# Two-pass put-back of expert rows: 0/1 matrix, weights applied at eviction, 14-unit spacing of whole units

## Chip, cores and metric

The kernel runs on one core of a Trainium2 chip. The metric is the device time of one execution in microseconds (us). A timed run is one number; a profiled execution also has a span, from its first to its last instruction, and a trace. Five engines work side by side: TensorE (PE in the rows; its weight loads stand apart as PEld), VectorE (DVE), ScalarE (ACT), GpSimd (POOL) and SyncE (SP), whose queue starts the transfers of the weights.

## The reference, cut to what matters

Two blocks run one after the other on 256 tokens of 1024 features. The change lies in the last part of the second block, a mixture of 32 experts: each token picks one group of eight experts, and in it two experts, whose outputs are added with two weights.

```python
def _hierarchical_moe(h, w_group, w_expert, w_gate, w_up, w_down):
    n, d = h.shape                                   # 256 tokens, 1024
    group_prob = jax.nn.softmax((h @ w_group).astype(jnp.float32), axis=-1)
    group = jnp.argmax(group_prob, axis=-1)
    group_gate = jnp.take_along_axis(group_prob, group[:, None], axis=1)
    ...
    top_p, top_local = lax.top_k(jax.nn.softmax(exp_logits, axis=-1), TOP_K)
    top_p = top_p / jnp.sum(top_p, axis=-1, keepdims=True)
    weight = (group_gate * top_p).reshape(-1)
    ...
    def expert_block(args):
        xb, e = args
        return (jax.nn.silu(xb @ w_gate[e]) * (xb @ w_up[e])) @ w_down[e]

    y = lax.map(expert_block, (buf.reshape(n_blocks, MOE_BLOCK, d), block_expert)).reshape(cap, d)
    contrib = y[dest] * w_sorted[:, None].astype(y.dtype)
    return jnp.zeros((n, d), y.dtype).at[tok_sorted].add(contrib)

# in second_block, after it:
    x = x + gate_ffn[:, None, :] * y
    return _rmsnorm(x, g_final)
```

## The kernel before, in words

**Units.** All weights are laid out as units of 128x2048 float32 (1 MB). SP's queue loads them in the order of `PLAN` (L304), into tiles called `raw`. An expert has six: two each of `eg` (gate), `eu` (up) and `ed` (down), so the 32 experts have 192. A unit is split before use: ACT writes its rounded part `hi` (a copy to the type fp32r, L221), DVE the rest `lo` (L348), and PE multiplies with both (`convert_unit`, `rows_times`). A *whole* unit is not split: PE reads `raw` itself in full float32, and ACT and DVE have nothing to do for it. Function `whole` picks them among the experts' units: index 9 and every 20th after it, nine units in all.

**Slots.** One pool of `NS = 18` tiles of 1 MB holds raw units, split units (two each), the tokens' rows (`hth`, `htl`), the state `x` and the experts' outputs. `prefetch` starts a load when fewer than `st["cap"]` raw units are held (6 in this stage) and a slot is free. `take_unit` splits up to two units ahead of the one in use.

**Pairs.** Experts go in pairs p, each with 32 slots per expert. For pair p the loop runs `gate_up` (PE banks `pe`), `hidden` (bank `pT`, then the product with silu, `sgm` and `hsz`), and `down` (banks `pd`), where `down` of pair p-1 stands between the `gate_up` of pair p and p+1. ACT evicts `pe` and later `pd` to a tile `gy` (two pairs share a 1 MB slot). `gather` (bank `pg`) fetches the tokens' rows for four pairs at a time.

**Put-back.** After every fourth pair `put_back` adds the four pairs' rows to the tokens. For each of eight feature blocks and each pair, PE multiplies 128 rows of `gy` with `wsel`, a 128x256 matrix that holds a token's weight in the row of its slot and nought elsewhere, into bank `py`, all in float32; DVE adds the result, scaled by `mod`, to `x` (L1598). `put_weights` makes `wsel` two pairs earlier: DVE writes it by tokens (`gw`), PE transposes it (bank `pw`, L1502), ACT evicts it (`ws`). There are put-backs of four, four, four, three and one pair; the last is in the tail, ahead of the final norm.

**Order.** Work that is not tied to a unit is a generator in the list `bg`; `pull` takes one step of it at each half unit, `post` puts an eviction some half units later, and `drain` runs out what is left. The framework then settles where each engine's instructions stand.

Of the kernel before, what the change touches and what calls it, by code (L numbers as in the profile page):

```python
# [213 lines left out]
def block_kernel(ctx: ExitStack, tc: tile.TileContext, A, out):  # L214
# [5 lines left out]
    def act(out, in_, func, **k):  # L220
        ins = S.activation(out, in_, func, **k).ins  # L221
        last["act" if func in (AF.Copy, AF.Identity, AF.Square, AF.Abs) else "func"] = ins
        return ins
# [12 lines left out]
    def mm(*a, **k):  # L236
        last["mm"] = T.matmul(*a, **k).ins  # L237
# [13 lines left out]
    def unit(name, dt=F32):  # L251
        live[0] += 1
        assert live[0] <= NS, (name, live)
        return units.tile([P, 2048], dt, name=name, tag="u")

    def free(n=1):
        live[0] -= n
# [4 lines left out]
    def t512(name, dt=F32):  # L262
        return tpool[0].tile([P, 512], dt, name=name, tag="t")
# [7 lines left out]
    def k2v(t):  # L271
        return t.rearrange("p (k t) -> p k t", k=2)
# [17 lines left out]
    def whole(u):  # L290

        if u < MOE0:
            return PLAN[u][0] == "v" or PLAN[u][0] == "conv" and PLAN[u][1] in (2, 5)
        m = u - MOE0
        return m < NU - MOE0 - 4 and m % 20 == 9

    def prefetch(upto=-1):
        while st["dma"] < NU and ((len(raw) < st["cap"] and live[0] < NS) or st["dma"] <= upto):
# [104 lines left out]
    def post(fn, n=1):  # L403
        due.append((st["step"] + n, fn))
# [35 lines left out]
    def drain():  # L440
        while bg or bg2:
            pull(1000)
# [843 lines left out]
    first.close()  # L1286
    moe = ctx.enter_context(ExitStack())
    pairs = moe.enter_context(tc.tile_pool(name="pairs", bufs=3, reuse_waits="tile"))
    tpool[0] = moe.enter_context(tc.tile_pool(name="wide2", bufs=5, reuse_waits="tile"))
    st["mconv"] = MOE0  # L1290
    convert_unit(2)
    acc = ps("ss")
# [159 lines left out]
    def choose(g):  # L1452

        oh = ohs[g] = [pairs.tile([P, 256], F32R, name="oh", tag="oh", bufs=4) for tt in range(2)]
        for tt in range(2):
            t1 = t256("oh1")
            V.tensor_scalar(t1, slot, slg[g][:, 0, tt:tt + 1], None, op0=OP.is_equal)
            last["oh"] = V.scalar_tensor_tensor(oh[tt], slot, slg[g][:, 1, tt:tt + 1], t1,
                                                op0=OP.is_equal, op1=OP.add).ins
            yield  # L1460
# [16 lines left out]
            post(keep, 1)  # L1477
            yield

    def put_weights(g):  # L1480

        gw = [t512("gw") for tt in range(2)]
        for tt in range(2):
            t = [t256("gw1") for i in range(2)]
            for i in range(2):
                V.tensor_scalar(t[i], slot, slg[g][:, i, tt:tt + 1], wt[:, i, tt:tt + 1],
                                op0=OP.is_equal, op1=OP.mult)
            g4 = gw[tt].rearrange("p (e i r) -> p e i r", e=8, i=2)
            t3 = [v.rearrange("p (e r) -> p e r", e=8) for v in t]
            for i in range(2):  # L1490
                V.tensor_tensor(g4[:, :, i], t3[0], t3[1], op=OP.add)
            yield
            yield
        for _ in range(6):
            yield
        wsel[g] = pairs.tile([P, 1024], F32, name="ws", tag="ws", bufs=1).rearrange("p (q t) -> p q t", q=4)
        for q2 in range(2):
            p = ps("pw")
            for i in range(2):
                for tt in range(2):  # L1500
                    q = 2 * q2 + i
                    T.transpose(p[:, i * 256 + tt * 128:i * 256 + (tt + 1) * 128],  # L1502
                                gw[tt][:, q * 128:(q + 1) * 128], ident)
            post(lambda p=p, q2=q2: act(wsel[g][:, 2 * q2:2 * q2 + 2].rearrange("p q t -> p (q t)"), p,
                                                 AF.Copy), 2)
            yield

    gy = {}

# [6 lines left out]
                       start=a and j == 0, stop=z and j == len(ws) - 1, skip_group_check=True)  # L1516
        return run

    pes, gyu = {}, {}

    def window(t, e):
        return t[:, (e % 2) * 64:(e % 2) * 64 + 128]
# [1 line left out]
    def gate_up(e):  # L1524
        x4 = xs[e // 4 % 2][:, :, e // 2 % 2]
        q, odd = e // 2, e % 2 == 1
        if not odd:
            pes[q] = [ps("pe"), ps("pe")]
        for i, nm in enumerate(("eg", "eu")):
            p = pes[q][i]  # L1530
            for k2 in range(2):
                for ws in take_unit(nm, e, k2):
                    rows_times([(p, window(x4[:, 4 * k2 + k], e), k, not odd and k2 + k == 0, odd and k2 + k == 4)
                                for k in range(4)])(ws)
        if odd:
            if q % 2 == 0:
                g = unit("gy")
                gy[q], gy[q + 1] = g[:, :1024], g[:, 1024:]
            for i in range(2):
                post(lambda i=i, p=pes[q][i]: act(gy[q][:, i * 512:(i + 1) * 512], p, AF.Copy), i + 2)  # L1540

    def hidden(q):

        t = gy[q]
        p = ps("pT")
        for f in range(8):
            mm(p[:, f * 64:(f + 1) * 64], t[:, f * 128:(f + 1) * 128], fold, start=True, stop=True)
        sg = t256("sgm")
        hs = hsz[q % 2]
        sv = sg.rearrange("p (f e r) -> p f e r", f=4, e=2)  # L1550
        ho = hs.rearrange("p f (h i r) -> p f h i r", h=3, i=2)

        def product():
            act(sg, p[:, 0:256], AF.Silu)
            V.tensor_mul(sg, p[:, 256:512], sg)

        def parts():
            act(ho[:, :, 0:3:2, 0], sv, AF.Copy)
            V.tensor_sub(ho[:, :, 0:3:2, 1], sv, ho[:, :, 0:3:2, 0])  # L1559
        post(product, 2)  # L1560
        post(parts, 4)
        return hs
# [3 lines left out]
    def down(e, hs):  # L1566
        odd = e % 2 == 1
        if not odd:
            pds[:] = [ps("pd"), ps("pd")]
        for k2 in range(2):  # L1570
            for ws in take_unit("ed", e, k2):
                rows_times([(pds[n], window(hs[:, 2 * k2 + i], e), 2 * i + n, not odd and k2 + i == 0,
                             odd and k2 + i == 2) for i in range(2) for n in range(2)])(ws)
        if odd:
            y = gy[e // 2]

            def keep(pd=list(pds)):
                for n in range(2):
                    if n and e == NE - 1:
                        V.tensor_copy(y[:, n * 512:(n + 1) * 512], pd[n])  # L1580
                    else:
                        act(y[:, n * 512:(n + 1) * 512], pd[n], AF.Copy)
            post(keep, 2)

    def put_back(qs, after=None):

        for f2 in range(4):
            p = ps("py")
            for i in range(2):
                f = 2 * f2 + i  # L1590
                for n, q in enumerate(qs):
                    mm(p[:, i * 256:(i + 1) * 256], gy[q][:, f * 128:(f + 1) * 128],
                       wsel[q // 4][:, q % 4], start=n == 0, stop=n == len(qs) - 1)

            def add(f2=f2, p=p):
                for i in range(2):
                    f = 2 * f2 + i
                    V.scalar_tensor_tensor(x[:, f], p[:, i * 256:(i + 1) * 256], mod[:, 40 + f:41 + f], x[:, f],  # L1598
                                           op0=OP.mult, op1=OP.add)
            if after:  # L1600
                after(add)
            else:
                post(add, 3)
            yield
        for q in qs:
            gy.pop(q)
            if q % 2:
                free()

    st["hold"] = held  # L1610
    st["cap"] = 6
# [8 lines left out]
    with tc.issue_after(last["oh"]):  # L1620
        weights()
    for p in range(NE // 2 + 1):
        if p < NE // 2:
            gate_up(2 * p)
        if p:
            if p == NE // 2:
                flush()
                drain()
                flush()
                st["order"] = 0  # L1630
            hs = hidden(p - 1)
            if p == NE // 2:
                flush()
        if p < NE // 2:
            gate_up(2 * p + 1)
            if p % 4 == 3 and p // 4 < 3:
                drain()
                bg.append(gather(p // 4 + 1))
                st["bg"] = 2
            if p % 4 == 2:  # L1640
                bg.append(put_weights(p // 4))
                if p // 4 < 3:
                    bg.append(choose(p // 4 + 1))
        if p:
            for e in (2 * p - 2, 2 * p - 1):
                down(e, hs)
            if st["bg"] == 2:
                drain()
                st["bg"] = 1
            if p % 4 == 0 and p < NE // 2:  # L1650
                post(lambda p=p: bg.insert(0, put_back([p - 4, p - 3, p - 2, p - 1])), 3)
            elif p == NE // 2 - 1:
                post(lambda p=p: bg.insert(0, put_back([p - 3, p - 2, p - 1])), 3)
    flush()
# [127 lines left out]
```

## Time and profile before

| what | us |
|---|---|
| timed runs, median of 3 (lowest, highest) | 1255.14 (1254.77, 1258.93) |
| the profiled execution's own time | 1256.86 |
| its span | 1255.1 |
| PE busy in the span | 1193.1 (95%) |
| DVE busy | 1016.1 (81%) |
| ACT busy | 789.7 (63%) |

Shares over the whole span mix stages that have different limits. The experts take the last 515 us or so (from about 740), and that stage is read by stretches: for each, the busy time of every engine, the share of time in which the DMA engines moved data, and the rate in GB/s. The mean granted TensorE clock of the span is 0.979 of full speed.

### The profile page before, as it was taken

How to read it: one execution, taken by the hardware profiler on the slowest of the kernel's cores; microseconds unless marked ns; L12 is line 12 of the kernel's file. 1: busy time of each engine (PE TensorE's matmuls, PEld its weight loads, DVE VectorE, ACT ScalarE, POOL GpSimd, SP SyncE). 2: the span in 40 equal slices, each digit the busy share in tenths (PEclk: the TensorE clock that was granted, in tenths of full speed). 3: DMA queues.
4: the chain of work that ended last, by engine and by line, in shares of the span. 5: the costliest groups of instructions: out<-in, count | busy, mean ns of one | idle time of the engine just before them, and what ended most of it. 6: DMA issues, size and time to landing. Idle time of an engine off the chain costs nothing.

```text
span 1255.1 us, 18668 instructions
## 1 busy us (share of the span) xinstructions
PE 1193.1 (95%) x7396; PEld 1040.2 (83%) x7396; DVE 1016.1 (81%) x1212; ACT 789.7 (63%) x908; POOL 102.0 (8%) x106
## 2 busy tenths in 40 slices
PE   7989899999999999988999999999999999999996
PEld 6984899999999999978898977777777776778774
DVE  6796799977798988676746689998898979888985
ACT  6465545465654444455455478897778867876873
POOL 1769200210000000000000000000000000000000
PEclk8999899999999999988899989999999999999998
DMA  9634347436877897423106229999999989998971
GB/s 362 265 110 181 113 173 269 159 115 270 348 287 299 339 336 285 194 101 135 68 8 263 101 93 424 421 421 421 370 421 421 421 322 424 421 417 323 423 319 36
DMA packets 48620, 341.20 MB, mean 272 GB/s; under 512 B 5392, under 2 KB 5648, under 8 KB 7824
## 3 DMA queue, kind: packets, MB, share of 16 engines
q1 hardware_dynamic: 47664, 337.65, 68.0%
q10 hardware_dynamic: 864, 2.31, 0.5%
q8 instruction: 60, 0.98, 0.3%
q14 instruction: 32, 0.26, 0.1%
HBM read 338.88 MB, written 1.05 MB: 271 GB/s over the span
## 4 chain that ended last, share of the span: by engine, by line
PE 70%; DVE 14%; ACT 8%; issue 5%; POOL 2%; DMA 1%; SPq 0%; DVEq 0%; ACTq 0%; POOLq 0%
PE pe L237 12%; DVE lo L348 7%; PE pd L237 5%; PE pbr L237 5%; PE fo L237 5%; PE pfg L237 5%; PE pfu L237 5%; PE py L237 4%; PE pq L237 4%; PE po L237 4%; PE pgt L237 4%; ACT hi L221 4%; PE pc L237 2%; PE z L237 2%; PE pg L237 2%
## 5 line engine op out<-in xcount | busy, mean ns | idle before, releaser
L221 ACT ACTIVATE hi<-raw 128x1024 fp32r<-128x1024 f32 (+1 forms) x379 | 549.8, 1471 | 306.3 <-issue 54.2
L348 DVE TENSOR_TENSOR lo<-raw,hi 128x2048 fp32r<-128x2048 f32 (+1 forms) x185 | 410.9, 2262 | 50.2 <-ACT hi L221 37.2
L327 DVE TENSOR_TENSOR lo<-raw,hi 128x1024 fp32r<-128x1024 f32 x194 | 243.3, 1262 | 87.1 <-ACT hi L221 83.1
L237 PE MATMUL pe<-lo,xs 128*128 128x512 f32 x488 | 136.4, 404 | 9.5 <-DVE lo L348 9.1
L237 PE MATMUL pe<-hi,xs 128*128 128x512 f32 x488 | 136.4, 403 | 1.0 <-ACT hi L221 0.7
L237 PEld LDWEIGHTS pe<-lo,xs 128*128 128x128 f32 x488 | 89.0, 188 | 36.7 <-DVE lo L348 18.7
L237 PEld LDWEIGHTS pe<-hi,xs 128*128 128x128 f32 x488 | 90.4, 188 | 25.5 <-ACT hi L221 3.0
L650 DVE SCALAR_TENSOR_TENSOR ca<-ch,par,ca 128x255 f32<-128x255 f32 (+25 forms) x180 | 94.0, 555 | 1.0
L237 PE MATMUL pd<-lo,hsz 128*128 128x512 f32 x244 | 69.0, 404 | 4.0 <-DVE lo L348 3.0
L237 PE MATMUL pd<-hi,hsz 128*128 128x512 f32 x244 | 68.3, 401 | 1.2 <-DVE hsz L1559 1.2
L237 PEld LDWEIGHTS pd<-lo,hsz 128*128 128x128 f32 x244 | 43.4, 188 | 20.7 <-DVE lo L348 12.7
L237 PE MATMUL py<-ws,gy 128*128 128x256 f32 x256 | 57.4, 380 | 2.2 <-ACT gy L221 2.2
L237 PE MATMUL pgt<-nh,hi 128*128 128x256 f32 x192 | 55.8, 290 | 1.9 <-ACT vt L221 1.9
L237 PEld LDWEIGHTS pd<-hi,hsz 128*128 128x128 f32 x244 | 45.9, 188 | 13.5 <-issue 3.0
L316 DVE SCALAR_TENSOR_TENSOR raw<-raw,aux 128x1024 f32<-128x1024 f32 x48 | 56.8, 1218 | 0.0
L237 PEld LDWEIGHTS py<-ws,gy 128*128 128x128 f32 x256 | 48.4, 190 | 10.0 <-ACT gy L221 3.1
L641 POOL TENSOR_TENSOR ca<-ca,tap 128x255 f32<-128x255 f32 (+29 forms) x60 | 54.0, 901 | 21.4 <-ACT tap L221 17.7
L237 PE MATMUL pgt<-nh,lo 128*128 128x256 f32 x192 | 55.3, 288 | 0.0
L237 PE MATMUL pgt<-nl,hi 128*128 128x256 f32 x192 | 55.1, 287 | 0.0
L237 PE MATMUL pfg<-xh,hi 128*128 128x256 f32 x176 | 49.9, 284 | 0.0
L237 PE MATMUL pfg<-xl,hi 128*128 128x256 f32 x176 | 49.7, 283 | 0.0
L237 PE MATMUL pfg<-xh,lo 128*128 128x256 f32 x176 | 49.7, 282 | 0.0
(347 smaller groups left out, 2866.2 us busy)
## 6 DMA issues: line engine op xcount, KB each, us to landing
raw<-in_ws_dram SPq DMA_DIRECT2D x318, 1024.0 KB, 8.6
x<-in_xt_dram SPq DMA_DIRECT2D x4, 256.0 KB, 4.5
raw<-in_ws_dram SPq DMA_DIRECT2D x2, 512.0 KB, 9.0
out_dram<-xo SPq DMA_DIRECT2D x4, 256.0 KB, 2.9
aux<-in_sguw_dram ACTq DMA_DIRECT2D x1, 512.0 KB, 9.5
aux<-in_cnt_dram SPq DMA_DIRECT2D x1, 512.0 KB, 12.6
aux<-in_sgub_dram ACTq DMA_DIRECT2D x1, 512.0 KB, 3.8
aux<-in_cvec_dram ACTq DMA_DIRECT2D x1, 512.0 KB, 4.8
```

Of the source, the lines that this page charges most:

```text
L221: ins = S.activation(out, in_, func, **k).ins
L237: last["mm"] = T.matmul(*a, **k).ins
L316: V.scalar_tensor_tensor(r, r, 1.0, cond["c"], op0=OP.mult, op1=OP.mult, accum_out=mod[:, col:col + 1])
L327: st["lo"] = V.tensor_sub(lo, r, hi).ins
L348: st["lo"] = V.tensor_sub(lo[:, c], raw[u][:, c], hi[:, c]).ins
L641: G.tensor_tensor(ca[:, j, d:], ca[:, j, d:], t[:, :256 - d], op=OP.add)
L650: V.scalar_tensor_tensor(ca[:, j, d:], ch[:, j, :256 - d], w(30 - d), ca[:, j, d:], op0=OP.mult, op1=OP.add)
```

## The change

`wsel` becomes a matrix of noughts and ones of type fp32r. The weight of a row, summed over the tokens, goes to a column `wrow`, and each pair's `pd` is multiplied by it when it is evicted. That eviction makes two parts, as for the weights: ACT writes the rounded half `yh` of a tile `y`, DVE the rest `yl`. `put_back` then multiplies both parts, in fp32r, with the same 0/1 matrix. A pair's `y` now takes a slot of its own from `down` on; the eviction of `pe` goes to a tile `gu` outside the slots.

`put_weights` is cut in two: `weigh` (DVE) runs with the first pair of a group of four, `turn_weights` (PE's transposes, then DVE instead of ACT evicts) right behind the put-back of the group before, because the weights are now needed at the first eviction. The cap on raw units goes 5, 5, 7, 6 with the pair's place in its group. Whole units come every 14th (13 in all). The pool for 128x512 tiles has three buffers instead of five.

```diff
@@ whole
-        return m < NU - MOE0 - 4 and m % 20 == 9
+        return m < NU - MOE0 - 4 and m % 14 == 9
-    tpool[0] = moe.enter_context(tc.tile_pool(name="wide2", bufs=5, reuse_waits="tile"))
+    tpool[0] = moe.enter_context(tc.tile_pool(name="wide2", bufs=3, reuse_waits="tile"))
...
@@ put_weights, now weigh and turn_weights
-            post(lambda p=p, q2=q2: act(wsel[g][:, 2 * q2:2 * q2 + 2].rearrange("p q t -> p (q t)"), p,
-                                                 AF.Copy), 2)
+            def keep(p=p, q2=q2):
+                V.tensor_scalar(wsel[g][:, 2 * q2:2 * q2 + 2].rearrange("p q t -> p (q t)"), p, 0.0, None,
+                                op0=OP.not_equal)
+                V.tensor_reduce(wrow[g][:, 2 * q2:2 * q2 + 2], k2v(p), axis=AX.X, op=OP.add)
+            post(keep, 2)
...
@@ down
-            y = gy[e // 2]
+            q = e // 2
+            y = unit("y", F32R)
+            gy[q] = y[:, :1024], y[:, 1024:]
+            w = wrow[q // 4][:, q % 4:q % 4 + 1]
             def keep(pd=list(pds)):
                 for n in range(2):
-                    if n and e == NE - 1:
-                        V.tensor_copy(y[:, n * 512:(n + 1) * 512], pd[n])
-                    else:
-                        act(y[:, n * 512:(n + 1) * 512], pd[n], AF.Copy)
+                    yh, yl = (v[:, n * 512:(n + 1) * 512] for v in gy[q])
+                    act(yh, pd[n], AF.Copy, scale=w)
+                    V.scalar_tensor_tensor(yl, pd[n], w, yh, op0=OP.mult, op1=OP.subtract)
...
@@ put_back
-                    mm(p[:, i * 256:(i + 1) * 256], gy[q][:, f * 128:(f + 1) * 128],
-                       wsel[q // 4][:, q % 4], start=n == 0, stop=n == len(qs) - 1)
+                    for z, y in enumerate(gy[q]):
+                        mm(p[:, i * 256:(i + 1) * 256], y[:, f * 128:(f + 1) * 128],
+                           wsel[q // 4][:, q % 4], start=n + z == 0, stop=n == len(qs) - 1 and z == 1)
...
@@ the loop over pairs p
+        st["cap"] = (5, 5, 7, 6)[p % 4] if p else 6
+        if p % 4 == 0 and p < NE // 2:
+            bg.append(weigh(p // 4))
+            if not p:
+                bg.append(turn_weights(0))
...
+            if p % 4 == 1:
+                drain()
...
-                post(lambda p=p: bg.insert(0, put_back([p - 4, p - 3, p - 2, p - 1])), 3)
+                def back(p=p):
+                    bg[:0] = [put_back([p - 4, p - 3, p - 2, p - 1]), turn_weights(p // 4)]
+                post(back, 3)
```

The first place is PE at the first put-back (four pairs). Before, with one row for each float32 matrix product (the trace counts two instructions for one):

```order
L237 MATMUL pe<-hi,xs 128x512 x4
L237 MATMUL py<-ws,gy 128x256 x9
L237 MATMUL pe<-lo,xs 128x512 x4
L237 MATMUL pe<-hi,xs 128x512 x4
L237 MATMUL pe<-lo,xs 128x512 x4
L237 MATMUL pe<-hi,xs 128x512 x4
L237 MATMUL py<-ws,gy 128x256 x18
L237 MATMUL pe<-lo,xs 128x512 x4
L237 MATMUL py<-ws,gy 128x256 x5
```

And now:

```order
L237 MATMUL pe<-hi,xs 128x512 x4
L237 MATMUL py<-ws,y 128x256 x18
L237 MATMUL pe<-lo,xs 128x512 x4
L237 MATMUL pe<-hi,xs 128x512 x4
L237 MATMUL pe<-lo,xs 128x512 x4
L237 MATMUL pe<-hi,xs 128x512 x4
L237 MATMUL py<-ws,y 128x256 x10
L237 MATMUL pe<-lo,xs 128x512 x4
L237 MATMUL py<-ws,y 128x256 x18
L1509 MATMUL pw<-cst,gw 128x128 x4
L237 MATMUL py<-ws,y 128x256 x18
```

The 32 float32 products became 64 fp32r ones, and the transposes `pw` of the next four pairs' weights, which stood two pairs later, now stand within them (four more follow a unit later).

The second place is DVE around the same put-back. Before:

```order
L348 TENSOR_TENSOR lo<-raw,hi 128x2048 x9
L1598 SCALAR_TENSOR_TENSOR x<-py,mod,x 128x256 x2
L348 TENSOR_TENSOR lo<-raw,hi 128x2048
L1598 SCALAR_TENSOR_TENSOR x<-py,mod,x 128x256 x4
L348 TENSOR_TENSOR lo<-raw,hi 128x2048
L1598 SCALAR_TENSOR_TENSOR x<-py,mod,x 128x256 x2
L1555 TENSOR_TENSOR sgm<-pT,sgm 128x256
```

And now:

```order
L1597 SCALAR_TENSOR_TENSOR y<-pd,wrow,y 128x512 x2
L348 TENSOR_TENSOR lo<-raw,hi 128x2048 x2
L1614 SCALAR_TENSOR_TENSOR x<-py,mod,x 128x256 x2
L348 TENSOR_TENSOR lo<-raw,hi 128x2048
L1614 SCALAR_TENSOR_TENSOR x<-py,mod,x 128x256 x4
L348 TENSOR_TENSOR lo<-raw,hi 128x2048
L1614 SCALAR_TENSOR_TENSOR x<-py,mod,x 128x256 x2
L1514 TENSOR_SCALAR ws<-pw 128x512
L1516 TENSOR_REDUCE wrow<-pw 128x2
L1514 TENSOR_SCALAR ws<-pw 128x512
L1516 TENSOR_REDUCE wrow<-pw 128x2
```

DVE gains the two parts `yl` of the last pair ahead of the put-back, and four evictions of `pw` behind it; a pair of `y<-pd` stands once in every other pair too.

## Rows read from the trace of the kernel before

**Rows 1.** Windows: stretch, its us; busy PE, PEld, DVE, ACT, POOL; PEclk; DMA share; GB/s.

```profile
739.80:867.70 127.90, 123.65 (x551) 93.86 (x550) 119.01 (x71) 113.14 (x102) 0.00 (x0) 1.00 0.97 401
...
867.70:905.00 37.30, 37.30 (x175) 31.50 (x174) 30.43 (x23) 24.90 (x18) 0.00 (x0) 1.00 0.97 378
905.00:995.00 90.00, 85.21 (x381) 63.66 (x380) 81.85 (x54) 76.10 (x70) 0.00 (x0) 1.00 1.01 421
995.00:1032.00 37.00, 37.00 (x167) 29.96 (x166) 27.22 (x22) 22.13 (x17) 0.00 (x0) 1.00 0.87 338
1032.00:1123.40 91.40, 86.53 (x389) 65.26 (x388) 84.56 (x54) 78.08 (x72) 0.00 (x0) 1.00 1.01 420
1123.40:1160.00 36.60, 36.60 (x172) 30.94 (x172) 28.36 (x22) 23.25 (x18) 0.00 (x0) 1.00 0.86 337
1160.00:1216.00 56.00, 54.27 (x249) 42.63 (x248) 55.15 (x36) 47.01 (x37) 0.00 (x0) 1.00 1.01 420
1216.00:1255.10 39.10, 25.47 (x114) 20.26 (x112) 20.14 (x28) 15.00 (x23) 1.62 (x1) 0.88 0.09 32
```

**Rows 2.** The chain that ended last, at the first put-back: start us, us, what.

```profile
867.89 3.88 PE py L237 x18
871.78 3.73 PE pe L237 x16
875.50 7.77 PE py L237 x36
...
884.20 2.16 PE py L237 x10
```

**Rows 3.** Timeline there, DVE and ACT: in brackets the idle time before and its releaser.

```profile
884.30 2.29 DVE L348 TENSOR_TENSOR lo<-raw,hi 128x2048 fp32r<-128x2048 f32 x1 [4.32 <-issue]
...
886.40 3.77 ACT L221 ACTIVATE hi<-raw 128x2048 fp32r<-128x2048 f32 x2 [5.27 <-PE py L237]
```

**Rows 4.** The chain in the first block: fp32r products of 256 columns, back to back.

```profile
406.77 5.70 PE pfg L237 x48
```

**Rows 5.** Timeline of PE: a whole unit's products, and transposes of the weights.

```profile
1018.87 3.60 PE L237 MATMUL pe<-raw,xs 128*128 128x512 f32 x8
...
811.10 0.82 PE L1502 MATMUL pw<-cst,gw 128*128 128x128 f32 x6
```

**Rows 6.** Groups by form: count, busy us, mean ns of one, idle before.

```profile
L348 DVE TENSOR_TENSOR lo<-raw,hi 128x2048 fp32r<-128x2048 f32 x181 | 406.2, 2286 | 49.5 <-ACT hi L221 36.6 <-issue 10.2 <-PE pd L237 2.2
...
L1486 DVE TENSOR_SCALAR gw<-cst,rt 128x256 f32<-128x256 f32 x16 | 6.2, 405 | 0.0
L1491 DVE TENSOR_TENSOR gw<-gw,gw 128x256 f32<-128x256 f32 x16 | 6.0, 417 | 0.0
...
L1164 DVE TENSOR_REDUCE mx<-z 128x1 f32<-128x256 f32 x8 | 3.3, 413 | 0.0
L1397 DVE SCALAR_TENSOR_TENSOR row<-pT,rt,dg 128x512 f32<-128x512 f32 x4 | 3.0, 745 | 0.0
L1580 DVE COPY gy<-pd 128x512 f32<-128x512 f32 x1 | 0.7, 691 | 4.9 <-PE pd L237 4.9
...
L221 ACT ACTIVATE ws<-pw 128x512 f32<-128x512 f32 x8 | 4.3, 584 | 0.0
```

**Rows 7.** DMA issues of the experts' stage: KB each, median us from issue to landing.

```profile
raw<-in_ws_dram SPq DMA_DIRECT2D x181, 1024.0 KB, 10.9
```

**Rows 8.** Timeline of the tail: PE, ACT and DVE.

```profile
1220.96 7.17 PE L237 MATMUL py<-ws,gy 128*128 128x256 f32 x32 [1.77 <-ACT gy L221]
...
1235.38 0.60 ACT L221 ACTIVATE gy<-pd 128x512 f32<-128x512 f32 x1 [8.56 <-PE pd L237]
...
1237.19 3.47 DVE L1598 SCALAR_TENSOR_TENSOR x<-py,mod,x 128x256 f32<-128x256 f32 x8 [0.89 <-PE py L237]
```

**Rows 9.** Timeline: the last products of a `pd`, and ACT's eviction of it.

```profile
865.76 1.21 PE L237 MATMUL pd<-lo,hsz 128*128 128x512 f32 x4
...
869.92 1.06 ACT L221 ACTIVATE gy<-pd 128x512 f32<-128x512 f32 x2
```

More of the change, by code (lines that the diff above doesn't have):

```diff
@@ L1478, in gather, with weigh @@
             yield
-    def put_weights(g):
-        gw = [t512("gw") for tt in range(2)]
+    gws, wrow = {}, {}
+    def weigh(g):
+        gw = gws[g] = [t512("gw") for tt in range(2)]
         for tt in range(2):
@@ L1495, in put_weights, with turn_weights @@
             yield
-        wsel[g] = pairs.tile([P, 1024], F32, name="ws", tag="ws", bufs=1).rearrange("p (q t) -> p q t", q=4)
+    def turn_weights(g):
+        gw = gws.pop(g)
+        wsel[g] = pairs.tile([P, 1024], F32R, name="ws", tag="ws", bufs=1).rearrange("p (q t) -> p q t", q=4)
+        wrow[g] = tmp.tile([P, 4], F32, name="wrow", tag="wrow", bufs=2)
         for q2 in range(2):
@@ L1503, in put_weights @@
                                 gw[tt][:, q * 128:(q + 1) * 128], ident)
-            post(lambda p=p, q2=q2: act(wsel[g][:, 2 * q2:2 * q2 + 2].rearrange("p q t -> p (q t)"), p,
-                                                 AF.Copy), 2)
+            def keep(p=p, q2=q2):
[3 more added lines that the diff above has]
+            post(keep, 2)
             yield
+        yield
+        yield
+        yield
     gy = {}
@@ L1517, in rows_times @@
         return run
-    pes, gyu = {}, {}
+    pes, gus = {}, {}
     def window(t, e):
@@ L1535, in gate_up @@
         if odd:
-            if q % 2 == 0:
-                g = unit("gy")
-                gy[q], gy[q + 1] = g[:, :1024], g[:, 1024:]
+            gus[q] = pairs.tile([P, 1024], F32, name="gu", tag="gu", bufs=1)
             for i in range(2):
-                post(lambda i=i, p=pes[q][i]: act(gy[q][:, i * 512:(i + 1) * 512], p, AF.Copy), i + 2)
+                post(lambda i=i, p=pes[q][i]: act(gus[q][:, i * 512:(i + 1) * 512], p, AF.Copy), i + 2)
     def hidden(q):
-        t = gy[q]
+        t = gus.pop(q)
         p = ps("pT")
@@ L1606, in put_back @@
             gy.pop(q)
-            if q % 2:
-                free()
+            free()
     st["hold"] = held
@@ L1639, in block_kernel @@
                 st["bg"] = 2
[L1640 to L1643, printed above, removed]
+            if p % 4 == 2 and p // 4 < 3:
+                bg.append(choose(p // 4 + 1))
         if p:
+            if p % 4 == 1:
+                drain()
             for e in (2 * p - 2, 2 * p - 1):
```

## The prediction

> **What bounds the kernel now.** I read the stretches of the experts' stage first, cut at the three put-backs of four pairs [rows 1]. Between them (905 to 995, 1032 to 1123.4, 1160 to 1216) the DMA engines are busy all the time and move 420 to 421 GB/s: there the weights' arrival sets the pace, and a 1 MB unit (1.0486 MB) takes 1.0486/421 = 2.49 us. In the three stretches that begin with a put-back, the rate is 378, 338 and 337 GB/s, and PE is busy for the whole 37.3, 37.0 and 36.6 us. Had the DMA kept 421 GB/s, the same bytes would have come in 37.3 x 378/421 = 33.5, then 29.7 and 29.3 us. So these stretches lose 3.8, 7.3 and 7.3 us, together 18.4 us. That is all that can be won ahead of the tail: between the put-backs nothing can outrun the DMA.
>
> Then I read why. The chain that ended last runs on PE through the first put-back [rows 2]: 18 + 36 + 10 = 64 instructions in 3.88 + 7.77 + 2.16 = 13.81 us, 216 ns each. Meanwhile the next units can't be split, as the slots of split units come free only when PE has used them: ACT sat idle 5.27 us until PE was through with a `py`, and DVE 4.32 us at the same time [rows 3]. Unsplit units fill the raw slots, and the queue has none to load into.
>
> DVE is the engine to watch next. It is busy 81.85 of 90.0, 84.56 of 91.4 and 55.15 of 56.0 us between the put-backs, and only 30.4, 27.2 and 28.4 us in the stretches that begin with one [rows 1]. What it idles there (6.9, 9.8 and 8.2 us), it idles mostly because PE holds it up.
>
> **The change part by part.** *PE at the put-back.* 32 float32 products, two instructions each, become 64 fp32r ones. The nearest row has fp32r products of 256 columns back to back, 48 in 5.70 us, 119 ns each [rows 4]: 64 x 119 ns = 7.6 us against 13.8, 6.2 us less for four pairs. The transposes move into this stretch: six took 0.82 us [rows 5], so eight take at most 1.1 us. Net 5.1 us less. PE was busy throughout, so its need falls to 32.2, 31.9 and 31.5 us.
>
> *DVE's evictions.* Each pair gains two `yl`: the nearest row is the same operation, from PSUM, of the same size, 745 ns [rows 6]; 1.5 us a pair. Each group of four gains two `not_equal` passes over 128x512 of PSUM (a copy of that size took 691 ns) and two sums over as much: the nearest sum, over half as much, took 413 ns, so each lies between 413 and 826 ns, and I take 0.69 us as for the copy. That is 2.8 us, and 4.3 us with the one pair that falls into a put-back stretch. DVE's need there becomes 34.7, 31.5 and 32.7 us. ACT loses 2 x 584 ns a group and wins nothing by it: it has room already (24.9 of 37.3 us).
>
> *Whole units.* Four more units are not split: 2.29 us less on DVE [rows 6], and PE needs 3.60 instead of 8 x 233 ns = 1.87 us, 1.7 us more [rows 2, 5]. Counting along `PLAN`, one now falls into each put-back stretch (indices 65, 107, 163), where before only the second had one (109). So the first and third have PE 33.9 and 33.2 us, DVE 32.4 and 30.4. Between the put-backs PE has 4.8 us and more to spare, so the others cost nothing there.
>
> *The put-back stretches, summed.* The largest need: first PE 33.9 (DMA 33.5, DVE 32.4), second PE 31.9 (DVE 31.5, DMA 29.7), third PE 33.2 (DVE 30.4, DMA 29.3). Where engines lie that close they still stop for each other; DVE reached 55.15 of 56.0 us, 98.5%, in the last full-rate stretch, so I divide the first two by that: 34.4, 32.4, 33.2. Gain 2.9 + 4.6 + 3.4 = **10.9 us**. Bounds: if the put-back's work spreads over its neighbours, where PE has room, the DMA sets the time and the gain is 18.4 us; if all of DVE's present pauses stay and its new work comes on top, the stretches grow by 2.0 + 4.3 + 2.0, a loss of 8.3 us. I am nearer the first, as the pauses have a cause that shrinks: the 4.32 us stood behind 36 instructions at 216 ns, which are now pieces of 10 and 18 at 119.
>
> *A saturated engine takes on more.* The Trainium skill ("Perfetto Trace Analysis", section "Optimizing Scalar/DVE Operations") says that where DVE is saturated, handing some of its work to ScalarE may make sense; the change hands DVE two evictions a group that ACT did. By that rule 2 x 0.69 = 1.4 us would be better left where they were. The rows agree that DVE is the fuller engine (30.4 against 24.9 us in the first put-back stretch), but PE decides there, and the sum stays as it is.
>
> *Between the put-backs.* DVE gains 3 x 1.5 = 4.5 us for three pairs, and in the second stretch has one split less: 86.4 of 90.0 and 86.8 of 91.4 us, under 98.5%, hidden behind the DMA. In the last it gains 3.0 for two pairs and loses a group's `gw`, 4 x 0.405 + 4 x 0.417 = 3.3 us [rows 6], which now comes before the put-back: 54.9 of 56.0, also hidden. Ahead of the first put-back it gains 4.5, the 2.8 of the first group, and a `gw` more, less one split: 119.0 + 8.3 = 127.3 of 127.9 us. At 98.5% that takes 129.2: **+1.3 us**. As `weigh` and `turn_weights` of the first group also stand at the very start, with nothing in hand yet, **+1 us** more (0 to their 2.8).
>
> *Three 128x512 buffers instead of five.* The four `row` tiles at the start can't all be held, and one waits for an earlier one's split: **+0.5 us**, between 0 and one such operation, 0.745 [rows 6].
>
> *Slots.* `y` takes four slots where `gy` took three at the put-back, hence the cap of 5 there. A load takes 10.9 us from issue to landing [rows 7], 4.4 units' time; a slot less is a unit less that can arrive while PE is held up, 0 to 2.49 us for each put-back. I take 0, since the DMA stays busy while any unit is in flight; the other end is a rival. On SP's queue nothing moves.
>
> *Tail.* The put-back of three pairs had 32 instructions in 7.17 us on PE, after a wait for ACT's eviction [rows 8]; now 32 x 119 ns = 3.8, 3.4 us less, and the wait for two `yl` adds 1.5: **-1.9 us** (0 to -3.4). In the last put-back the adds began 1.8 us after ACT's eviction started and ran 3.47 us on DVE [rows 8]. Now two `yl` (1.5 us, behind a first `yh` of 0.60) stand ahead of them, so they begin at 2.1 us at the soonest, though PE needs 16 x 119 ns = 1.9 us where it took 3.5: **+0.3 us**.
>
> Sum: -10.9 + 1.3 + 1 + 0.5 - 1.9 + 0.3 = -9.7 us, from the profiled execution's own 1256.86: 1247.2. The median of the runs is 1.7 us below the profiled execution, so for a timed run I say **1245 us**.
>
> **The rivals.** *DVE's queue is held up by its own evictions (slower).* `yl` needs ACT's `yh`; the splits behind it on DVE wait with it, and PE for those. For it: PE was done with a `pd` at 866.97 and ACT came to it at 869.92, 3 us later, which cost DVE nothing as only ACT's queue stood in between [rows 9]. Against it: DVE trails ACT in the same order of units, so `yh` is mostly written before DVE reaches `yl`. It decides from 9.7/15 = 0.65 us of waiting at each of 15 evictions; at 1.5 us each it adds 22 us: 1267. 20%, for 1259 to 1270.
>
> *The bound only changes its engine (no change).* If DVE keeps half its pauses in the put-back stretches (3.4, 4.9, 4.1 us), it needs 35.8, 36.4 and 34.5: the gain is 1.5 + 0.6 + 2.1 = 4.2 in place of 10.9, and the time 1252. For it: DVE is at 91 to 98% in the neighbouring stretches. The smaller cap leads to about the same, 3 x 2.49 = 7.5 us given back: 1252.5. Together 20%, for 1251.4 to 1259.
>
> *The dips vanish.* At the bound of 18.4 us, and with the whole 3.4 us of the tail, it is 1236. For it: PE has 4.8 and 4.9 us to spare after each put-back, about what it would have to put off. 12%.
>
> **How the numbers follow.** The forecast, 1239 to 1251, has 48%, vanished dips (1234 to 1239) 12%. A measurement of this kernel can tell about 0.3%, 3.8 us, from no change: faster means under 1251.4, slower over 1258.9. Faster 48 + 12 = 60%, same 20%, slower 20%. The range goes from 1234 to 1261, where the slower case has only begun; that leaves some 17% out, nearly all of it above.
>
> **What would show it.** Right: `py` at some 119 ns an instruction, 7.6 us for four pairs; over 370 GB/s in the stretches after a put-back; `yl` at 0.75 us each. Wrong: DVE idle ahead of `yl` for ACT by over 0.65 us each; a rate between put-backs under 415 GB/s with DVE busy all the time; or longer waits of the load queue in the pairs with cap 5.

## The result and the profile after

The change makes the kernel slower: 1264.49 us (median of 5 runs, 1263.34 to 1266.56) against 1255.14 (5 runs, 1253.56 to 1258.93), a ratio of 1.0070 with a 95% interval of 1.0057 to 1.0084. The prediction, 1245 us with a range of 1234 to 1261, is wrong in sign and misses the range.

The same windows as [rows 1], cut at the changed kernel's own put-backs (columns as there):

```profile
739.80:871.20 131.40, 121.52 (x534) 92.64 (x533) 121.19 (x81) 107.78 (x93) 0.00 (x0) 0.99 0.98 397
871.20:908.50 37.30, 35.21 (x190) 28.69 (x189) 36.01 (x30) 26.41 (x21) 0.00 (x0) 1.00 0.99 403
908.50:994.70 86.20, 81.42 (x367) 61.24 (x366) 81.56 (x58) 72.92 (x66) 0.00 (x0) 1.00 1.01 417
994.70:1031.70 37.00, 32.96 (x171) 26.75 (x170) 32.66 (x29) 22.73 (x17) 0.00 (x0) 0.91 0.92 357
1031.70:1128.10 96.40, 88.34 (x385) 66.02 (x385) 83.44 (x58) 74.67 (x68) 0.00 (x0) 0.98 0.97 391
1128.10:1164.70 36.60, 32.30 (x173) 27.43 (x172) 33.57 (x28) 23.11 (x18) 0.00 (x0) 0.91 0.92 349
1164.70:1221.00 56.30, 54.92 (x248) 41.42 (x247) 50.44 (x29) 45.82 (x34) 0.00 (x0) 1.00 1.00 412
1221.00:1262.40 41.40, 25.16 (x115) 19.23 (x114) 24.00 (x32) 15.84 (x24) 1.71 (x1) 0.82 0.09 31
```

The rate behind the put-backs rose from 378, 338, 337 to 403, 357, 349 GB/s, well short of 421. Between them, where it had been 420 to 421, it now falls too, to 391 in 1031.7 to 1128.1. No engine is full there (DVE 83.44 of 96.4 us, PE 88.34), so this is waiting, not saturation. The granted clock, 1.00 in every such stretch before, falls to 0.91 behind two put-backs.

PE's own part came as forecast. The chain at the first put-back, which answers to [rows 2]:

```profile
871.39 2.06 PE py L237 x18
873.45 3.66 PE pe L237 x16
877.11 1.18 PE py L237 x10
878.28 0.93 PE pe L237 x4
879.22 2.07 PE py L237 x18
881.72 2.07 PE py L237 x18
```

That is 64 instructions in 7.4 us, 115 ns each, where they took 13.81. But PE has new waits. The list of waits from 739 us on (us in total, times, longest):

```profile
PE pe L237 <- DVE lo L348: 17.0, 21, 2.3
PE pd L237 <- DVE hsz L1572: 14.4, 6, 3.9
DVE y L1597 <- ACT y L221: 3.3, 2, 2.5
```

Before, the first two of these were:

```profile
PE pe L237 <- DVE lo L348: 9.1, 14, 1.2
PE pd L237 <- DVE hsz L1559: 1.2, 1, 1.2
```

The one wait of `pd` for `hsz` stood ahead of the first put-back. Now 1.7, 3.9 and 3.9 of the 14.4 us stand in the pairs behind the three put-backs. DVE hardly waits for ACT's `yh` (3.3 us), so the rival that I had feared did not come. The timeline of DVE and PE in the pair behind the third put-back shows the longest of the new waits:

```profile
1146.01 0.87 DVE L1614 SCALAR_TENSOR_TENSOR x<-py,mod,x 128x256 f32<-128x256 f32 x2
1146.79 0.68 DVE L1514 TENSOR_SCALAR ws<-pw 128x512 fp32r<-128x512 f32 x1
1147.39 0.68 DVE L1516 TENSOR_REDUCE wrow<-pw 128x2 f32<-128x512 f32 x1
1147.99 0.69 DVE L1514 TENSOR_SCALAR ws<-pw 128x512 fp32r<-128x512 f32 x1
1148.59 0.68 DVE L1516 TENSOR_REDUCE wrow<-pw 128x2 f32<-128x512 f32 x1
1149.18 2.29 DVE L348 TENSOR_TENSOR lo<-raw,hi 128x2048 fp32r<-128x2048 f32 x1
...
1151.72 4.49 DVE L348 TENSOR_TENSOR lo<-raw,hi 128x2048 fp32r<-128x2048 f32 x2
...
1156.12 0.42 DVE L1572 TENSOR_TENSOR hsz<-sgm,hsz 128x256 fp32r<-128x256 f32 x1
...
1156.59 2.08 PE L237 MATMUL pd<-hi,hsz 128*128 128x512 f32 x4 [3.87 <-DVE hsz L1572]
1158.46 1.91 PE L237 MATMUL pd<-lo,hsz 128*128 128x512 f32 x4
...
1160.17 1.91 PE L237 MATMUL pd<-hi,hsz 128*128 128x512 f32 x4
1161.88 1.24 PE L237 MATMUL pd<-lo,hsz 128*128 128x512 f32 x4
```

Four evictions of `pw`, 2.7 us, stand on DVE ahead of the splits, and `hsz` stands behind those. PE waits 3.87 us for it. Then its next groups of four take 1.91 us, where the same four take 1.1 elsewhere: the windows over it show the granted clock at 0.50 of full speed, the 1.2 GHz level:

```profile
1151.00:1157.00 6.00, 1.71 (x6) 1.08 (x6) 6.00 (x6) 5.38 (x6) 0.00 (x0) 0.86 0.98 395
1157.00:1162.00 5.00, 5.00 (x13) 3.85 (x13) 5.00 (x3) 1.91 (x1) 0.00 (x0) 0.50 0.80 251
```

### The profile page after: what moved, and what is told of

Read it like the earlier page. It is cut to its first block, busy times and chain, and to the rows that moved or that the text cites. A ratio compares the mean times of both kernels' runs of the same rounds, so it can differ in the third digit from the quotient of the medians.

```text
span 1262.4 us, 18709 instructions
## 1 busy us (share of the span) xinstructions
PE 1176.4 (93%) x7396; PEld 1021.9 (81%) x7396; DVE 1036.7 (82%) x1255; ACT 782.9 (62%) x897; POOL 102.4 (8%) x106
## 3 DMA queue, kind: packets, MB, share of 16 engines
q10 hardware_dynamic: 864, 2.31, 0.5%
## 4 chain that ended last, share of the span: by engine, by line
PE 66%; DVE 16%; ACT 7%; issue 6%; POOL 3%; DMA 1%; SPq 0%; DVEq 0%; ACTq 0%; POOLq 0%
PE pe L237 12%; DVE lo L348 8%; PE pd L237 7%; PE pbr L237 5%; PE fo L237 5%; PE pfu L237 5%; PE pfg L237 5%; PE pq L237 4%; PE po L237 4%; PE pgt L237 4%; ACT hi L221 3%; PE pg L237 2%; PE z L237 2%; PE py L237 2%; DVE ca L650 2%
## 5 line engine op out<-in xcount | busy, mean ns | idle before, releaser
L221 ACT ACTIVATE hi<-raw 128x1024 fp32r<-128x1024 f32 (+1 forms) x375 | 542.7, 1467 | 305.7 <-issue 50.8
L348 DVE TENSOR_TENSOR lo<-raw,hi 128x2048 fp32r<-128x2048 f32 (+1 forms) x181 | 402.4, 2263 | 39.1 <-ACT hi L221 34.4
L237 PE MATMUL pe<-lo,xs 128*128 128x512 f32 x476 | 131.5, 402 | 17.3 <-DVE lo L348 17.0
L237 PE MATMUL pe<-hi,xs 128*128 128x512 f32 x476 | 132.3, 403 | 0.5 <-ACT hi L221 0.5
L237 PEld LDWEIGHTS pe<-lo,xs 128*128 128x128 f32 x476 | 86.3, 189 | 44.6 <-DVE lo L348 28.2
L237 PE MATMUL pd<-hi,hsz 128*128 128x512 f32 x240 | 72.7, 428 | 14.4 <-DVE hsz L1572 14.4
L237 PEld LDWEIGHTS pd<-lo,hsz 128*128 128x128 f32 x240 | 45.4, 200 | 18.9 <-DVE lo L348 10.3
L237 PE MATMUL fo<-fl,hi 128*128 128x256 f32 x176 | 49.4, 283 | 0.0
L237 PE MATMUL pfu<-xh,hi 128*128 128x256 f32 x176 | 49.3, 280 | 0.0
```

Of the source, the lines that this page charges most:

```text
L348: st["lo"] = V.tensor_sub(lo[:, c], raw[u][:, c], hi[:, c]).ins
```

## The experiments

The theories. **D**: DVE's added work (`yl`; `ws` and `wrow` in place of ACT's eviction) costs the time. Rivals: **S**, the slots and caps cost it; **W**, the whole units do. After the first four runs, D was split: **P**, the place of the `pw` evictions, ahead of `hsz`; **A**, their amount, wherever they stand. Ratios are to the kernel before, run beside each; 0.001 is 1.26 us.

**Caps alone.** The kernel before with

```diff
+        st["cap"] = (5, 5, 7, 6)[p % 4] if p else 6
```

> The kernel before with only the caps on raw units of the changed one (5, 5, 7, 6 in place of 6). The changed kernel took 1264.5 against 1255.1. Theory S (slots): the smaller cap in the pairs around a put-back starves the load queue, and the loss is there; then this kernel is 5 us or more slower than before, 1260 or above. Theory D (VectorE's queue): the loss comes from the work that VectorE took on; then the caps alone cost next to nothing, 1253 to 1258.

1258.61 us, 1.0035 (1.0018 to 1.0052). On a kernel whose put-backs still hold the slots up, a smaller cap costs 4 us (between the two ranges expected); I had set this at nothing.

**Whole units alone.** The kernel before with `m % 14`.

> The kernel before with only 13 whole units in place of 9. Theory W (whole units): they fall into the put-back stretches, where TensorE has no room, at 1.7 us each, and hold raw slots longer: 1258 to 1264. Theory D: VectorE saves four splits (9 us in all) which it can use: 1251 to 1256.

1258.57 us, 1.0025 (1.0013 to 1.0036), in the range of W: they cost 3 us on this kernel, where PE fills the put-back stretches.

**No `yl`.** The changed kernel without that line; `put_back` multiplies `yh` twice, so the rows are added with twice their rounded part.

> The changed kernel without VectorE's 32 operations for yl; TensorE multiplies yh twice, so it has as many products as before, and the rows are added with twice the rounded part. Theory D: VectorE loses 24 us of work that stands ahead of splits and hsz, and the time falls below that of the kernel before: 1236 to 1248. Theory S and W: the loss stays, 1260 or above.

1252.67 us, 0.9987 (0.9975 to 0.9999): 32 instructions of 0.745 us are worth 0.0083, 10 us. The sign is D's, but the time lies above the range expected for it. From 739 us on PE waits 14.8 us for `lo` and 10.7 for `hsz` here, against 17.0 and 14.4 with `yl`.

**No `ws` on DVE.** ACT evicts `pw` as before, with the weights in it, and each `pd` is multiplied by one:

```diff
-                V.tensor_scalar(wsel[g]..., p, 0.0, None, op0=OP.not_equal)
-                V.tensor_reduce(wrow[g]..., k2v(p), axis=AX.X, op=OP.add)
+                act(wsel[g]..., p, AF.Copy)
...
-            w = wrow[q // 4][:, q % 4:q % 4 + 1]
+            w = one1[:, q % 4:q % 4 + 1]
```

> The changed kernel with the eviction of pw on ScalarE as before and no sums (the matrix keeps the weights, the eviction of pd multiplies by one; so the products are rounded). VectorE loses 11 us, all of it just ahead of hsz in the pair behind a put-back, where TensorE waited 1.7, 3.9 and 3.9 us for hsz and then ran at half its clock. Theory D: these waits go, 1250 to 1258. Theory S and W: 1262 or above.

1251.10 us, 0.9972 (0.9955 to 0.9988): 0.0098, 12 us, for 10.9 us of DVE's work (16 x 0.68). PE's wait for `hsz` falls from 14.4 to 4.4 us. So D holds, and dearer than its busy time. The next two look for why.

**The evictions later.** The changed kernel with `turn_weights` not right behind the put-back, but started behind `hidden` with 5 steps in hand; the work is the same, and half of the evictions now stand behind `hsz`.

> The changed kernel with turn_weights half a pair later, so that only half of its evictions stand ahead of hsz on VectorE, with the same work in all. Theory P (place): what costs is where these evictions stand, as they delay hsz, TensorE waits and loses its clock; then much of the 13 us that went with them goes here too, 1252 to 1259. Theory A (amount): VectorE has too much work wherever it stands, 1261 to 1266.

1256.57 us, 1.0011 (0.9995 to 1.0027), in the range of P.

**Later still:** 7 steps, so that all four stand behind `hsz` on DVE.

> The changed kernel with the transposes of the weights moved behind the pair's hidden product, so far that all four evictions of their banks (not_equal and sum, twice) stand behind hsz on VectorE instead of ahead of it; the work is the same. Place (theory P: the 13 us that the eviction of the weights costs are mostly PE's waits for hsz and the half clock behind them): no wait of pd for hsz over 1 us, no matmuls of pd at the half rate in the pair behind a put-back, 1252 to 1257. Amount (theory A: the 2.8 us of VectorE per group cost their time wherever they stand): 1260 to 1265.

1254.55 us, 0.9996 (0.9980 to 1.0013). The waits there, and DVE and PE behind the third put-back:

```profile
PE pd L237 <- DVE hsz L1575: 5.0, 3, 3.1
```

```profile
1146.65 0.41 DVE L1575 TENSOR_TENSOR hsz<-sgm,hsz 128x256 fp32r<-128x256 f32 x1
...
1147.49 1.08 PE L237 MATMUL pd<-hi,hsz 128*128 128x512 f32 x4
...
1151.39 0.68 DVE L1517 TENSOR_SCALAR ws<-pw 128x512 fp32r<-128x512 f32 x1
```

`hsz` is 14.4 - 5.0 = 9.4 us less waited for, `pd` runs at 1.08 us for four at once, and the time falls by 0.0074, 9 us. (I had expected no such wait over 1 us; the longest of those left, 3.1, stands at 769, behind the first pair, where this run changes nothing.) So of the 12 us of the eviction, about 9 are place: P. The other 3 (0.9996 against 0.9972, with intervals that touch) are at the edge of what these runs can tell.

**Whole units taken back.** The changed kernel with `m % 20`.

> The changed kernel with nine whole units as before in place of 13. Theory A: VectorE lacks the time for four more splits (9 us), 1266 to 1274. Theory W (a whole unit costs more than the split it saves, as in the kernel before, where 13 took 3 us longer than nine): 1259 to 1263.

1264.27 us, 1.0087 (1.0056 to 1.0118): between the two ranges, and nothing to tell from the change itself. The same in the run without `ws` on DVE:

> The kernel with pw evicted by ScalarE and no sums (1251.1) with nine whole units in place of 13. Theory A: 1253 to 1260, as VectorE is still the fullest engine. Theory W: 1246 to 1250.

1256.83 us, 1.0007 (0.9989 to 1.0024), in the range of A: there the four extra whole units are worth 0.0035, 4 us. W is no cause of the loss.

**Neither `ws` on DVE nor `yl`** (rows added with twice their rounded part).

> Both of the removals at once: pw evicted by ScalarE without sums, no yl, TensorE multiplying yh twice (rows added with twice the rounded part). Each alone took 12 and 13 us from the changed kernel. Theory A: the parts add up as VectorE is relieved of all its new work, 1236 to 1244. Theory P: the second one finds the place already free and gives little, 1247 to 1252.

1242.79 us, 0.9891 (0.9859 to 0.9923). `yl` costs 0.0081 here and 0.0083 above, `ws` 0.0096 and 0.0098: the two parts add up, as A expected and P did not. So P tells what the evictions cost, but not `yl`: that costs the same with the evictions gone. No run moved `yl` alone, and whether it costs by its place in DVE's queue, by its amount or by holding the bank of `pd` longer is open.

**`yl` on GpSimd.** ACT evicts `pd` a second time as float32, GpSimd subtracts:

```diff
-                    V.scalar_tensor_tensor(yl, pd[n], w, yh, op0=OP.mult, op1=OP.subtract)
+                    t = t512('yt')
+                    act(t, pd[n], AF.Copy, scale=w)
+                    G.tensor_tensor(yl, t, yh, op=OP.subtract)
```

> The version in which ScalarE evicts the weights' banks (no wrow, factor one), and in which VectorE loses yl too: ScalarE writes the product pd*w once more into a float32 tile, and GpSimd subtracts yh from it. It computes the reference. Theory D (VectorE's added work is what costs): as VectorE loses all that the change gave it, nearly as fast as the run without both, 1243 to 1247. Rival: GpSimd is slow or the extra eviction of ScalarE (32 x 0.68 us) and the later release of pd's bank give it back: 1249 to 1256.

1265.19 us, 1.0072 (1.0055 to 1.0089): beyond even the rival's 1256. GpSimd's group, and DVE beside it on the timeline:

```profile
L1597 POOL TENSOR_TENSOR y<-yt,y 128x512 fp32r<-128x512 f32 x32 | 66.3, 2088 | 464.8 <-ACT yt L221 412.6 <-DVE lo L348 52.2
```

```profile
843.04 0.73 DVE L1488 TENSOR_SCALAR gw<-cst,rt 128x256 f32<-128x256 f32 x2
...
845.81 2.63 POOL L1597 TENSOR_TENSOR y<-yt,y 128x512 fp32r<-128x512 f32 x2 [30.45 <-ACT yt L221]
845.89 1.41 DVE L1488 TENSOR_SCALAR gw<-cst,rt 128x256 f32<-128x256 f32 x1
...
847.22 1.84 DVE L1493 TENSOR_TENSOR gw<-gw,gw 128x256 f32<-128x256 f32 x2
848.99 0.40 DVE L1488 TENSOR_SCALAR gw<-cst,rt 128x256 f32<-128x256 f32 x1
```

While GpSimd works, DVE's `gw` takes 1.41 us where it takes 0.40 just after. From 739 us on, the splits take 401.6 us in all (393.2 in the run without `ws` alone) and `gw` 14.9 (9.9), so 13.4 of the 22.5 us that left DVE come back, and ACT has 21.9 us more. Which of the two the loss is made of was not told apart. The Trainium skill ("Perfetto Trace Analysis", section "Optimizing Scalar/DVE Operations") warns that handing work from DVE to GpSimd might not help, as the two share a read port of SBUF; the stretched rows agree.

**PE's part alone.** The kernel before with the rows and `wsel` in fp32r and each product done twice (rows added with twice their rounded part); no `yl`, no `wrow`; caps, whole units and places of the weights' work as before. Three more edits of the change are in it: `pe` is evicted to `gu` outside the slots, the rows take their slot (still one for two pairs) at `down` instead of at `gate_up`, and the 128x512 tiles have three buffers. So the rows hold two slots at a put-back, where they hold three in the kernel before and four in the changed one:

```diff
@@ gate_up
-                g = unit("gy")
+            gus[q] = pairs.tile([P, 1024], F32, name="gu", tag="gu", bufs=1)
...
@@ down
+                g = unit("gy", F32R)
...
@@ put_back
-                    mm(p[:, i * 256:(i + 1) * 256], gy[q]..., wsel[q // 4][:, q % 4], ...)
+                    for z in range(2):
+                        mm(p[:, i * 256:(i + 1) * 256], gy[q]..., wsel[q // 4][:, q % 4], ...)
```

> The kernel before with PE's part of the change alone: the put-back's products in fp32r at 64 for four pairs, each product twice with the same rounded rows (the rows are added with twice their rounded part: that part of the result is changed), no yl, no wrow, whole units, caps and places of the weights as before. If the gain that the prediction saw on PE is there (10.9 us in the put-back stretches, 3.4 in the tail): 1240 to 1246, and over 370 GB/s in the stretches behind a put-back. If PE's gain is itself lost (VectorE or ScalarE holds the splits up anyway): 1249 to 1255.

1231.59 us, 0.9812 (0.9789 to 0.9834): 24 us, far more than the 14 (10.9 and 3.4) that the prediction saw in it, and below both expectations. How much of it is PE's and how much the slot that is freed was not told apart. Its windows, first to third put-back and what follows each:

```profile
863.90:900.00 36.10, 36.02 (x188) 29.32 (x187) 34.20 (x25) 28.69 (x22) 0.00 (x0) 1.00 1.02 422
900.00:977.00 77.00, 72.45 (x335) 55.34 (x334) 69.49 (x48) 65.38 (x62) 0.00 (x0) 1.00 1.01 420
977.00:1013.00 36.00, 35.79 (x184) 28.65 (x184) 32.29 (x23) 26.42 (x21) 0.00 (x0) 1.00 1.01 421
...
1100.00:1136.00 36.00, 36.00 (x193) 30.25 (x192) 32.12 (x24) 27.99 (x20) 0.00 (x0) 1.00 1.01 420
```

The dips are gone. The changed kernel has this same put-back, so some 32 us of other costs are in it. Of these, `yl` and `ws` are known; 0.9891 - 0.9812, 10 us, was open. Three runs take it apart, each on top of this one.

**PE's part, and 13 whole units:**

> The run of PE's part alone (rows added with twice their rounded part) with a whole unit every 14th instead of every 20th. Theory W (four more whole units cost where PE is nearly full): 1233.5 to 1236, as they cost 3 us on the kernel before. Rival (they cost nothing where PE has 10 us to spare at each put-back): 1230 to 1233.

1232.38 us, 0.9823 (0.9803 to 0.9844), 0.0011 more: nothing to tell.

**PE's part, and the caps** ("as before" in the expectation means as in the run of PE's part alone):

> The run of PE's part alone (rows added with twice their rounded part) with the caps 5, 5, 7, 6 but the slots as before. If the cap itself costs (fewer loads in flight): 1235 to 1240. If only the slots that the rows take cost: 1230 to 1234.

1232.76 us, 0.9833 (0.9805 to 0.9860): 0.0021, within both intervals.

**PE's part, the caps and a slot for each pair's rows** (half of it unused), so that the rows hold four slots at a put-back instead of two:

> The run of PE's part alone (rows added with twice their rounded part) with the slots of the change: each pair's rows take a slot of their own from down on (half of it unused here), and the caps on raw units go 5, 5, 7, 6. Theory S (the slots are what the 11 us between this part alone and the run without both of VectorE's edits are made of): 1238 to 1243, with rates under 400 GB/s in the pairs ahead of and behind a put-back. Rival (slots cost little; the places of the weights' work cost it): 1231 to 1235.

1240.73 us, 0.9890 (0.9869 to 0.9911): two slots more cost 10 us with their caps, and 7 us (0.0057) against the run with the caps alone: S. Against the three slots of the kernel before no run prices them. Of the rates, only the 394 below is under 400 as expected. (The caps of before with these slots weren't tried: they ask for a 19th slot.) Its windows from the second put-back on:

```profile
977.00:1013.00 36.00, 35.37 (x182) 27.96 (x181) 32.66 (x24) 26.77 (x21) 0.00 (x0) 1.00 0.99 394
1013.00:1100.00 87.00, 82.15 (x376) 62.60 (x374) 80.36 (x52) 74.52 (x70) 0.00 (x0) 1.00 1.01 415
1100.00:1140.00 40.00, 38.19 (x195) 30.85 (x195) 33.94 (x25) 30.38 (x23) 0.00 (x0) 1.00 0.99 403
```

The first of these windows with the caps alone:

```profile
977.00:1013.00 36.00, 35.38 (x182) 27.94 (x181) 32.48 (x24) 26.55 (x21) 0.00 (x0) 1.00 1.01 418
```

PE and DVE are as full in both, yet with the slots the DMA moves less.

**One pass.** PE's part with each product done once: rows and weights are rounded to fp32r at their eviction, and no smaller part is added.

> The run of PE's part alone with each product done once, 32 fp32r instructions for four pairs: the experts' rows and their weights are rounded once to fp32r when they are evicted, and no smaller part is added. Half the products of that run, so PE has 3.8 us less at each put-back of four pairs; as the DMA engines were busy there already, only the tail can gain (2 to 4 us): 1227 to 1231. If PE still bounds the put-backs: 1218 to 1226.

1227.93 us (1226.44 to 1229.39), 0.9780 (0.9760 to 0.9801), the fastest of all and in the first range. It gives up the part that `yl` carries; where rows rounded once will do, the second pass, its eviction and its slots can go.

What ACT's split waits for is a sign of the bound of each kernel: PE's use of a slot, or data from the DMA. The waits of four kernels from 739 or 740 us on: before,

```profile
ACT hi L221 <- PE pe L237: 35.7, 27, 3.7
ACT hi L221 <- DMA raw<-in_ws_dram: 3.5, 6, 1.4
```

PE's part with the slots,

```profile
ACT hi L221 <- PE pe L237: 37.7, 26, 3.4
ACT hi L221 <- DMA raw<-in_ws_dram: 6.5, 8, 2.4
```

PE's part alone,

```profile
ACT hi L221 <- PE pe L237: 16.2, 18, 2.0
ACT hi L221 <- DMA raw<-in_ws_dram: 16.2, 24, 2.8
```

and one pass:

```profile
ACT hi L221 <- DMA raw<-in_ws_dram: 34.1, 48, 3.1
ACT hi L221 <- PE pe L237: 8.6, 12, 1.7
```

## Why the prediction was wrong

The ladder of runs, by ratio x 1255: PE's part, with the rows' slot taken later, -23.6 us; two slots more and the caps +9.8; the weights' places, whole units and the factor together +0.1; `yl` +10.2; `ws` and `wrow` on DVE +12.3. That makes +8.8, the loss. By the intervals each rung is good to 3 to 5 us.

The step that failed is the price of DVE's new work: 22.5 us by the ladder, where the prediction's terms for it (+1.3, +1 and 1.5 in the tail) come to 3.8. Without it, PE's part with the change's slots and caps took 1240.7 us, inside the forecast of 1239 to 1251. Whether that agreement is luck is open. PE's part alone gained 23.6 us and the slots with their caps took 9.8 back, so two terms that were set too low may have cancelled; but that kernel holds one slot fewer than the kernel before, and no run has PE's part with three.

- **PE at the put-back**: right in size, 115 ns an instruction. I limited the gain to 10.9 us in the put-back stretches, as PE, DVE and DMA needs lay close. From the first put-back's first `py` to that of the three-pair put-back it took 339.6 us before, 320.4 in PE's part alone and 329.3 with the slots: gains of 19.2 and 10.3 us. The first is the case "the dips vanish", which I gave 12%, though with the slot that is freed in it; the second is the sum's 10.9.
- **The bound of 18.4 us**: called all that can be won ahead of the tail, but the stretch ahead of the first put-back, at 401 GB/s, was left out of it; by the same sum it loses 127.9 x (1 - 401/421) = 6.1 us. In PE's part alone the first `py` starts 3.8 us earlier.
- **Slots, taken as 0**: too low by what the runs show. The caps alone cost 4 us on the kernel before, and two slots more with the caps cost 10 on PE's part alone. I argued that the DMA stays busy while any unit is in flight; the windows of the run with the slots show 394 to 415 GB/s from 977 to 1140 us with no engine fuller. The bound that I kept, 3 x 2.49 = 7.5 us, priced the cap; by the runs on PE's part alone the cap is the small part (0.0021) and the slots that the rows take the large one (0.0057).
- **"Between the put-backs ... hidden behind the DMA"**: here DVE's price went wrong. I compared DVE's busy sum with the stretch (86.8 of 91.4 us) and called the rest hidden. The sums were nearly right, but an instruction added to a queue in order makes what stands behind it late, however much idle time there is elsewhere: PE waits 17.0 us for `lo` and 14.4 for `hsz`. For the evictions of `pw` the run with them later shows it; for `yl`, 10 us for 22.5 us of work, it is argued. The sign that I had named, a rate under 415 GB/s with DVE busy all the time, came by half: 391 GB/s, with DVE at 83.44 of 96.4.
- **`not_equal` and sums, 2.8 us a group**: the size was right (0.68 us each, 2.7), the place was not read. The listing of DVE's order in the section on the change shows the four evictions behind the adds; I did not follow what stands behind them, `hsz`, on which the whole `down` of the pair hangs. That costs about 9 of the 12 us.
- **The Trainium skill's rule** ("Perfetto Trace Analysis", section "Optimizing Scalar/DVE Operations"), to hand ScalarE work where DVE is saturated, I set aside for 1.4 us. The run that does so for `ws` (and drops the sums) gains 12 us, though DVE was not saturated by its share. The case is rather that of another sentence in the same section: engines that are not saturated, "but are causing bubbles on other engines". The bubble here is the 3.87 us on PE; the remedy that it names, smaller instructions, no run here tried.
- **Ahead of the first put-back**, +1.3, +1 and +0.5: from the first `pe` to the first `py` took 867.7 - 737.2 = 130.5 us before and 871.2 - 733.7 = 137.5 now, +7.0 (the first `py` comes 3.5 us later, as the first `pe` comes 3.5 us earlier). Of it 4.2 us are there without `yl` and `ws` too (868.1 - 733.4 = 134.7); with PE's part and the slots it is 862.1 - 732.2 = 129.9. Which of the weights' work at the start and the whole units it is wasn't told apart.
- **Tail, -1.9 +0.3**: from the three-pair put-back's first `py` to the end it takes 48.2 us (1214.2 to 1262.4) where it took 47.8 (1207.3 to 1255.1), so +0.4. PE's products there run in part at the lower clock (0.82 of full speed in the window from 1221.0 on; 0.88 in the last of [rows 1]). PE's part alone gains 3.8 us there (1184.3 to 1228.3), and without `yl` and `ws` it takes 44.8 (1196.1 to 1240.9): so `yl` and `ws` cost 3.4 us, where I had 1.5 for `yl`.
- **The rival that was to be slower** had the right sign and about the right time (1267), but a mechanism that did not occur: DVE waited for ACT 3.3 us in all. Not DVE was held up by its evictions, but PE by DVE's.

## What to carry to other kernels

An edit that takes work off the bound may be worth all of the dip; test it by itself, with nothing else changed, before adding what it seems to need. For each instruction added to an in-order queue, don't ask whether the engine has room in the stretch, but which instruction right behind it releases the bound, and how late that becomes. Buffers that live longer are a cost like busy time: read it from what the loader's consumers wait for, data or a free slot.

## What the runs showed of the hardware

- A pause of PE costs more than its length: behind 3.87 us idle the granted clock was 0.50 for the next 5 us, the 1.2 GHz level, and four products took 1.91 us in place of 1.1. The first four groups of `pd` took 6.5 us there (1156.59 to 1163.12) and 3.8 in the run with all evictions later (1147.49 to 1151.32). The clock fell behind a shorter pause too: 0.66 in the 5 us from 1107 on, where PE had waited 2.31 us for `lo`.
- GpSimd took 2.09 us on average (its spans are rough: 1.27 to 3.61, with a median of 1.44) for a 128x512 subtraction to fp32r, where DVE needs 0.745 for one with a factor, from PSUM; beside it a 128x256 operation of DVE took 1.41 us in place of 0.40.
